# State-matrix powers from size and angle in one pass, parameters loaded ahead of the tokens, a broadcast row loaded behind the weights

## The chip, the cores and the metric

The program runs on one core of a Trainium2 chip. Its engines are PE (TensorE, matrix products; PEld is its weight load), DVE (VectorE), ACT (ScalarE), POOL (GpSimd) and SP (SyncE, which here only issues transfers). Each engine takes its instructions in the order of its own queue, and waits at an instruction until the semaphores it names have come. The metric is device time in microseconds of one execution; lower is better.

## The reference

Two blocks of two layers each run one behind the other on 256 tokens of 1024 channels. The change lies in the first layer, in the mixer with a diagonal state space (S5). What matters of it:

```python
def s5_mixer(u, a_re, a_im, log_dt, b_re, b_im, c_re, c_im, ...):
    dt = jnp.exp(log_dt)[:, None]
    mag = jnp.exp(a_re * dt)
    ab_re = mag * jnp.cos(a_im * dt)
    ab_im = mag * jnp.sin(a_im * dt)
    ...                                   # bb = discretised b, from ab and a
    bu = einsum('blgh,gph->blgp', uf, bb)
    x = associative_scan(x[l] = ab * x[l-1] + bu[l])   # over 256 tokens, complex
    y = einsum('blgp,ghp->blgh', x_re, c_re) - einsum(..., x_im, c_im) + d * uf
    y = gelu(y)
    return y * sigmoid(y @ glu_w + glu_b)

# layer 0
mod = silu(c) @ mod_w[0] + mod_b[0]       # 6 x 1024: shifts, scales, gates
h = rms_norm(x, norm_g[0, 0]) * (1 + sc1) + sh1
proj = h @ ab_w_in                        # 512 columns for S5, 3 x 512 for attention
y = concat([s5_mixer(proj[:, :512]), attention(proj[:, 512:])]) @ ab_w_out
```

There are 32 groups of 64 states (two groups share the 128 partitions, so a state parameter is a tile of 128 x 16), and 16 channels in a group.

## The kernel before

A weight matrix product is computed to nearly fp32: the weight and the operand are split into a rounded part and a remainder (`split`, lines 418 and 419: ACT rounds, DVE subtracts), and PE adds three products, lines 443 to 445. The weights come in loads of 512 KB on SP's queue into a ring of five buffers (`raw`). PE's wide products are what fills most of the time.

The scan is not run token by token. Tokens are taken in blocks of 8. `ssm_params` makes, from the powers 0 to 8 of the state matrix, the matrices that lead from the tokens of a block to its end state (`tt_`, made from `st` by transposes, line 982), from the state before a block to its outputs (`qr`, `qi`), and from a block's tokens to its outputs (`kmat`, by way of a table `ktab` that goes out to memory and back on POOL's queue, lines 1010 and 1014, in eight transfers). `ssm` runs the recursion over the 32 block states in seven steps, on DVE (real part) and POOL (imaginary part), lines 1078 to 1082: three steps inside groups of four blocks, three that double the distance, and one that brings the result to all; they use the powers 8, 16, 24, 32, 64 and 128. Each half of a step waits for the other engine's half of the step before. `ssm_out` multiplies `X`, the states, with `qr` and `qi` (line 1113) and the tokens with `kmat` (line 1110), and brings the outputs back into order (line 1121); gelu and the gated product follow.

The modulation of the first layer is a product of PE with 16 loads of 512 KB (`modulation`, line 543), in two halves of eight; loads go by turns into `raw` and a ring of three, `mraw`. After each half its transposes (line 563) and a reduction (line 570) give shift and scale, `scaled` makes from the tokens the operand (`n`, line 718; its rounded part `hh`, line 722; its remainder `hl`, line 723), and PE multiplies the half of the S5 columns of `ab_w_in` with it. The later parts of the modulations are taken by DVE as sums over rows (`dotted_with`, line 517): a row of weights on each partition times `crow`, which is silu(c) broadcast to all partitions. `row` loads `crow` (512 KB on SP's queue, line 505) and puts silu on it (line 506, ACT, with its table load).

The order on each queue is set by a scheduler that works on the program as it is written, with its own model of times; `issue_after` holds what stands in it behind a named instruction, and SP's order is that of the program in the front. The front writes: the load of the first parameters (`par0`), the tokens (`xT`), the state parameters (`par2`), the identity; squares and sums of the tokens for the norm (lines 705, 710, 638), the rsqrt chain on DVE (lines 646 to 651) and its spread by PE (line 657); then `ssm_params` in pieces between the halves of the modulation.

Of the kernel before, what the change touches and what calls it, by code (L numbers as in the profile page):

```python
# [11 lines left out]
F32 = mybir.dt.float32  # L12
F32R = mybir.dt.float32r
I32 = mybir.dt.int32
AF = mybir.ActivationFunctionType
ALU = mybir.AluOpType
# [3 lines left out]
P = 128  # L20
# [333 lines left out]
class Net:  # L354
# [514 lines left out]
    def ssm_params(self, sp, spt):  # L869

        nc, d, dram = self.nc, self.d, self.dram
        G = 16
        v = nc.vector
        S = [P, G]

        def small(name):
            return spt.tile(S, F32, name=name)
# [4 lines left out]
        lr, li, mag, th = small("s_lr"), small("s_li"), small("s_mag"), small("s_th")  # L882
        v.tensor_tensor(lr, are, dt, op=ALU.mult)
        nc.scalar.activation(mag, lr, AF.Exp)
        v.tensor_tensor(li, aim, dt, op=ALU.mult)
        self.reduce_arg(th, li, S, "s_ra", spt)
        sn, cs, ab = small("s_sn"), small("s_cs"), small("s_ab")
        nc.scalar.activation(sn, th, AF.Sin)
        v.scalar_tensor_tensor(ab, th, -1.0, th, op0=ALU.mult, op1=ALU.max)
        v.tensor_scalar(ab, ab, -1.0, math.pi / 2, op0=ALU.mult, op1=ALU.add)  # L890
        nc.scalar.activation(cs, ab, AF.Sin)

        pr = sp.tile([P, 14, G], F32, name="pr")
        pi = sp.tile([P, 14, G], F32, name="pi")
        v.memset(pr[:, 0, :], 1.0)
        v.memset(pi[:, 0, :], 0.0)
        v.tensor_tensor(pr[:, 1, :], mag, cs, op=ALU.mult)
        v.tensor_tensor(pi[:, 1, :], mag, sn, op=ALU.mult)

        def cmul(o, n, a, b):  # L900

            t1 = self.t([P, 4, G], "s_t1", 1, pool=spt)[:, :n, :]
            br_, bi_ = (q[:, b : b + 1, :].to_broadcast([P, n, G]) for q in (pr, pi))
            ar_, ai_ = pr[:, a : a + n, :], pi[:, a : a + n, :]
            v.tensor_tensor(pr[:, o : o + n, :], ar_, br_, op=ALU.mult)
            v.tensor_tensor(t1, ai_, bi_, op=ALU.mult)
            v.tensor_tensor(pr[:, o : o + n, :], pr[:, o : o + n, :], t1, op=ALU.subtract)
            v.tensor_tensor(pi[:, o : o + n, :], ar_, bi_, op=ALU.mult)
            v.tensor_tensor(t1, ai_, br_, op=ALU.mult)
            v.tensor_tensor(pi[:, o : o + n, :], pi[:, o : o + n, :], t1, op=ALU.add)  # L910

        cmul(2, 1, 1, 1)
        cmul(3, 2, 1, 2)
        cmul(5, 4, 1, 4)
        cmul(9, 1, 8, 8)
        cmul(10, 2, 8, 9)
        cmul(12, 1, 11, 11)
        cmul(13, 1, 12, 12)
# [1048 lines left out]
```

## Time and profile before

| | before |
|---|---|
| time, median of 3 runs | 1439.99 us (1439.74 to 1444.86) |
| the profiled execution | 1446.99 us |
| its span, first to last instruction | 1445.0 us |
| mean granted clock of PE in it | 0.973 of full speed |
| PE busy | 1361.3 us (94%) |
| PEld, DVE, ACT, POOL busy | 1238.6, 1184.4, 837.5, 151.1 us |
| transfers | 311.88 MB, mean 216 GB/s |

All views are of that one execution, times counted from its first instruction. A row in order of time gives start, duration, engine, line, operation, tiles written and read with their shape, how often, and in brackets how long the engine had been idle before and who ended that. A row of the waits names who waited, who was waited for, and the total, the times and the longest in us. The granted clock is a share of full speed.

### The profile page before, as it was taken

How to read it: one execution, taken by the hardware profiler on the slowest of the kernel's cores; microseconds unless marked ns; L12 is line 12 of the kernel's file. 1: busy time of each engine (PE TensorE's matmuls, PEld its weight loads, DVE VectorE, ACT ScalarE, POOL GpSimd, SP SyncE). 2: the span in 40 equal slices, each digit the busy share in tenths (PEclk: the TensorE clock that was granted, in tenths of full speed). 3: DMA queues.
4: the chain of work that ended last, by engine and by line, in shares of the span. 5: the costliest groups of instructions: out<-in, count | busy, mean ns of one | idle time of the engine just before them, and what ended most of it. 6: DMA issues, size and time to landing. Idle time of an engine off the chain costs nothing.

```text
span 1445.0 us, 28181 instructions
## 1 busy us (share of the span) xinstructions
PE 1361.3 (94%) x10702; PEld 1238.6 (86%) x10702; DVE 1184.4 (82%) x2379; ACT 837.5 (58%) x1562; POOL 151.1 (10%) x204
## 2 busy tenths in 40 slices
PE   6988899999998899999989999999999899999997
PEld 3666799999995898999977779999999668999997
DVE  7967888878697697888769867999888978799954
ACT  5533676554474575665457645866556645776642
POOL 1053000101000000001004650000110000000000
PEclk9998999999998999999989999999999899999998
DMA  9567576888757558878635435577795556557660
GB/s 367 205 158 277 202 262 220 277 256 289 245 175 291 177 175 338 277 233 266 213 95 161 137 119 198 155 244 247 264 325 195 170 182 240 176 177 235 193 185 29
DMA packets 91988, 311.88 MB, mean 216 GB/s; under 512 B 10949, under 2 KB 13662, under 8 KB 91726
## 3 DMA queue, kind: packets, MB, share of 16 engines
q1 hardware_dynamic: 72830, 244.67, 50.7%
q0 software_dynamic: 17856, 64.36, 13.9%
q8 instruction: 84, 1.38, 0.4%
q10 hardware_dynamic: 1168, 1.06, 0.3%
q14 instruction: 50, 0.41, 0.1%
HBM read 308.73 MB, written 1.32 MB: 215 GB/s over the span
## 4 chain that ended last, share of the span: by engine, by line
PE 68%; issue 15%; DVE 10%; ACT 3%; DMA 3%; POOL 1%; DVEq 0%; SPq 0%; POOLq 0%; ACTq 0%
PE mm L443 18%; PE mm L445 18%; PE mm L444 18%; DVE lo L419 3%; PE mo L543 2%; ACT hi L418 1%; PE o L1565 1%; PE ax L1665 1%; DVE mraw L517 1%; DMA raw<-ab_in 1%; PE sx L638 1%; PE s L443 1%; PE s L444 1%; POOL mraw L515 1%; PE s L445 1%
## 5 line engine op out<-in xcount | busy, mean ns | idle before, releaser
L418 ACT ACTIVATE hi<-raw 128x1024 fp32r<-128x1024 f32 (+3 forms) x402 | 404.0, 1007 | 371.4 <-PE mm L444 285.4
L419 DVE TENSOR_TENSOR lo<-raw,hi 128x1024 fp32r<-128x1024 f32 (+3 forms) x402 | 464.1, 1161 | 121.3 <-ACT hi L418 119.5
L443 PE MATMUL mm<-hh,hi 128*128 128x256 f32 x1440 | 410.3, 288 | 14.0 <-ACT hi L418 6.4
L445 PE MATMUL mm<-hh,lo 128*128 128x256 f32 x1440 | 407.9, 285 | 5.7 <-DVE lo L419 5.7
L444 PE MATMUL mm<-hl,hi 128*128 128x256 f32 x1440 | 408.3, 285 | 1.6 <-DVE hl L1184 1.0
L443 PEld LDWEIGHTS mm<-hh,hi 128*128 128x128 f32 x1440 | 274.1, 192 | 34.7 <-issue 9.9
L445 PEld LDWEIGHTS mm<-hh,lo 128*128 128x128 f32 x1440 | 275.6, 192 | 8.4 <-DVE lo L419 6.7
L444 PEld LDWEIGHTS mm<-hl,hi 128*128 128x128 f32 x1440 | 275.5, 191 | 7.6 <-issue 3.6
L443 PE MATMUL mm<-ah,hi 128*128 128x256 f32 x704 | 199.1, 283 | 1.8 <-ACT hi L418 1.8
L445 PE MATMUL mm<-ah,lo 128*128 128x256 f32 x704 | 198.0, 282 | 2.2 <-DVE lo L419 2.0
L444 PE MATMUL mm<-al,hi 128*128 128x256 f32 x704 | 197.1, 281 | 0.0
L443 PE MATMUL mm<-zh,hi 128*128 128x258 f32 x608 | 173.7, 289 | 8.1 <-ACT zh L303 4.7
L515 POOL DMA_DIRECT2D mraw<-modt x120 | 64.1, 534 | 1096.1 <-DVE mraw L517 949.1
L445 PE MATMUL mm<-zh,lo 128*128 128x258 f32 x608 | 174.6, 288 | 0.9 <-DVE lo L419 0.7
L444 PE MATMUL mm<-zl,hi 128*128 128x258 f32 x608 | 174.0, 287 | 0.0
L517 DVE SCALAR_TENSOR_TENSOR mraw<-mraw,crow 128x1024 f32<-128x1024 f32 x120 | 145.9, 1226 | 5.7 <-DMA mraw<-modt 5.5
L445 PEld LDWEIGHTS mm<-ah,lo 128*128 128x128 f32 x704 | 132.5, 189 | 3.9 <-DVE lo L419 3.6
L443 PEld LDWEIGHTS mm<-ah,hi 128*128 128x128 f32 x704 | 132.8, 189 | 3.2 <-ACT hi L418 2.0
L444 PEld LDWEIGHTS mm<-al,hi 128*128 128x128 f32 x704 | 132.7, 189 | 1.0 <-issue 1.0
L443 PEld LDWEIGHTS mm<-zh,hi 128*128 128x128 f32 x608 | 117.1, 194 | 9.0 <-ACT zh L303 4.9
L445 PEld LDWEIGHTS mm<-zh,lo 128*128 128x128 f32 x608 | 117.2, 193 | 1.8 <-DVE lo L419 1.7
L444 PEld LDWEIGHTS mm<-zl,hi 128*128 128x128 f32 x608 | 117.9, 194 | 0.2 <-DVE zl L304 0.2
(427 smaller groups left out, 2119.8 us busy)
## 6 DMA issues: line engine op xcount, KB each, us to landing
raw<-up SPq DMA_DIRECT2D x132, 512.0 KB, 4.4
mraw<-modt POOLq DMA_DIRECT2D x120, 512.0 KB, 5.2
raw<-down SPq DMA_DIRECT2D x64, 512.0 KB, 4.4
raw<-mod SPq DMA_DIRECT2D x60, 512.0 KB, 5.2
raw<-gate SPq DMA_DIRECT2D x44, 512.0 KB, 4.7
raw<-down SPq DMA_DIRECT2D x32, 384.0 KB, 3.3
raw<-hy_in SPq DMA_DIRECT2D x24, 512.0 KB, 4.3
raw<-cm_in SPq DMA_DIRECT2D x16, 512.0 KB, 3.6
```

Source lines behind the costliest of these rows:

```text
L418: nc.scalar.activation(hi, src, AF.Copy)
L419: return nc.vector.tensor_tensor(lo, src, hi.bitcast(F32), op=ALU.subtract)
L443: nc.tensor.matmul(out, wh, xh, start=start, stop=False)
L444: nc.tensor.matmul(out, wh, xl, start=False, stop=False)
L445: self.last = nc.tensor.matmul(out, wl, xh, start=False, stop=stop)
L515: nc.gpsimd.dma_start(w, self.d[f"modt{layer}"][u])
L517: nc.vector.scalar_tensor_tensor(w, w, 1.0, row, op0=ALU.mult, op1=ALU.mult, accum_out=out[:, u : u + 1]))
L543: nc.tensor.matmul(acc[g * 32 : g * 32 + 32, :], wt, src, start=(g not in begun), stop=last)
L638: last = self.nc.tensor.matmul(st[:, c0 + t : c0 + t + 1], q[:, t * P : (t + 1) * P], self.ones[:, 0:1], start=(i == 0), stop=(i == len(sq ...
L1565: nc.tensor.matmul(o[i * 64 : i * 64 + 64], vals[:, k, c : c + 64], pt[i][:, k, :], start=(k == 0), stop=(k == 3))
L1665: nc.tensor.matmul(ps, m[:, k, m0 : m0 + P], src[:, k, s], start=(k == 0), stop=(k == 1))
```

## The change

The powers of the state matrix: before, the first power is made of size and angle (`mag`, `th`, 16 columns), and the others of it by complex products (`cmul`, seven calls of six DVE instructions). After, a table of the fourteen exponents is filled on POOL, size and angle of all powers are taken at once (224 columns, in the two buffers that `st1` uses later), and one exp, one reduction of the angle, one sine, one cosine and two products give them all. The state parameters (`par2`) are now loaded ahead of the tokens. `row(0)` stands behind the last modulation load that has been issued, `self.load`, where before it had no such hold.

```diff
--- before.py
+++ after.py
@@ -879,43 +879,31 @@
         are, aim = self.parall("ssm_a_re"), self.parall("ssm_a_im")
         dt = small("s_dt")
         nc.scalar.activation(dt, self.parall("ssm_log_dt"), AF.Exp)
-        lr, li, mag, th = small("s_lr"), small("s_li"), small("s_mag"), small("s_th")
+
+        powers = (0, 1, 2, 3, 4, 5, 6, 7, 8, 16, 24, 32, 64, 128)
+        N = len(powers)
+        kp = spt.tile([P, N], F32, name="s_kp")
+        for i, k in enumerate(powers):
+            nc.gpsimd.memset(kp[:, i : i + 1], float(k))
+        pr = sp.tile([P, N, G], F32, name="pr")
+        pi = sp.tile([P, N, G], F32, name="pi")
+        lr, li = small("s_lr"), small("s_li")
         v.tensor_tensor(lr, are, dt, op=ALU.mult)
-        nc.scalar.activation(mag, lr, AF.Exp)
         v.tensor_tensor(li, aim, dt, op=ALU.mult)
-        self.reduce_arg(th, li, S, "s_ra", spt)
-        sn, cs, ab = small("s_sn"), small("s_cs"), small("s_ab")
+        two = [self.t([P, 4, 8, 16], f"st1{n}", 2, pool=spt).rearrange("p a r h -> p (a r h)") for n in range(2)]
+        mag, th, sn, cs = (t[:, i * N * G : (i + 1) * N * G].rearrange("p (k g) -> p k g", g=G) for t in two for i in range(2))
+        each = lambda q: q[:, None, :].to_broadcast([P, N, G])
+        kb = kp[:, :, None].to_broadcast([P, N, G])
+        v.tensor_tensor(cs, kb, each(li), op=ALU.mult)
+        v.tensor_tensor(mag, kb, each(lr), op=ALU.mult)
+        nc.scalar.activation(mag, mag, AF.Exp)
+        self.reduce_arg(th, cs, [P, N, G], "s_ra", spt)
         nc.scalar.activation(sn, th, AF.Sin)
-        v.scalar_tensor_tensor(ab, th, -1.0, th, op0=ALU.mult, op1=ALU.max)
-        v.tensor_scalar(ab, ab, -1.0, math.pi / 2, op0=ALU.mult, op1=ALU.add)
-        nc.scalar.activation(cs, ab, AF.Sin)
-
-        pr = sp.tile([P, 14, G], F32, name="pr")
-        pi = sp.tile([P, 14, G], F32, name="pi")
-        v.memset(pr[:, 0, :], 1.0)
-        v.memset(pi[:, 0, :], 0.0)
-        v.tensor_tensor(pr[:, 1, :], mag, cs, op=ALU.mult)
-        v.tensor_tensor(pi[:, 1, :], mag, sn, op=ALU.mult)
-
-        def cmul(o, n, a, b):
-
-            t1 = self.t([P, 4, G], "s_t1", 1, pool=spt)[:, :n, :]
-            br_, bi_ = (q[:, b : b + 1, :].to_broadcast([P, n, G]) for q in (pr, pi))
-            ar_, ai_ = pr[:, a : a + n, :], pi[:, a : a + n, :]
-            v.tensor_tensor(pr[:, o : o + n, :], ar_, br_, op=ALU.mult)
-            v.tensor_tensor(t1, ai_, bi_, op=ALU.mult)
-            v.tensor_tensor(pr[:, o : o + n, :], pr[:, o : o + n, :], t1, op=ALU.subtract)
-            v.tensor_tensor(pi[:, o : o + n, :], ar_, bi_, op=ALU.mult)
-            v.tensor_tensor(t1, ai_, br_, op=ALU.mult)
-            v.tensor_tensor(pi[:, o : o + n, :], pi[:, o : o + n, :], t1, op=ALU.add)
-
-        cmul(2, 1, 1, 1)
-        cmul(3, 2, 1, 2)
-        cmul(5, 4, 1, 4)
-        cmul(9, 1, 8, 8)
-        cmul(10, 2, 8, 9)
-        cmul(12, 1, 11, 11)
-        cmul(13, 1, 12, 12)
+        v.scalar_tensor_tensor(th, th, -1.0, th, op0=ALU.mult, op1=ALU.max)
+        v.tensor_scalar(th, th, -1.0, math.pi / 2, op0=ALU.mult, op1=ALU.add)
+        nc.scalar.activation(cs, th, AF.Sin)
+        v.tensor_tensor(pr, mag, cs, op=ALU.mult)
+        v.tensor_tensor(pi, mag, sn, op=ALU.mult)
 
         nr, den, cr, ci, t = small("s_nr"), small("s_den"), small("s_cr"), small("s_ci"), small("s_t")
         v.tensor_scalar(nr, pr[:, 1, :], 1.0, None, op0=ALU.subtract)
@@ -1766,9 +1754,9 @@
         with self.tc.tile_pool(name="sp", bufs=1, reuse_waits="tile") as sp:
             ut = sp.tile([P, 4, T], F32, name="ut")
             with self.tc.tile_pool(name="spt", bufs=1, reuse_waits="tile") as spt, self.banks(mm=4, ax=1, s=1):
-                nc.sync.dma_start(x, d["xT"])
                 self.p2 = spt.tile([P, d["par2"].shape[1]], F32, name="p2")
                 nc.sync.dma_start(self.p2, d["par2"])
+                nc.sync.dma_start(x, d["xT"])
                 nc.sync.dma_start(self.ident, d["k_ident"])
                 sq = []
                 for k in range(DC):
@@ -1812,7 +1800,8 @@
                     for _ in params:
                         pass
             self.later(0, self.modulation(0, range(4, 7), cs, mods[:1]), 1.5)
-            row = self.row(0)
+            with self.tc.issue_after(self.load.ins):
+                row = self.row(0)
             self.pace(1.0)
             self.also(1, 0, 28, 40, row, mods[0])
             self.p1 = per.tile([P, d["par1"].shape[1]], F32, name="p1")
```

The scheduler places the rest anew. ACT, between the two halves of the modulation; `tt_` is the copy of a transposed table, `modsb` that of the modulation, `hh` the rounded operand. Before:

```order
L983 ACTIVATE tt__290<-s 128x8x64
L418 ACTIVATE hi<-raw 128x1024
L560 ACTIVATE modsb<-mo 128x512
L983 ACTIVATE tt__290<-s 128x8x64
L418 ACTIVATE hi<-raw 128x1024
L983 ACTIVATE tt__290<-s 128x8x64 x2
L722 ACTIVATE hh<-n,mod_78 128x256 x3
L418 ACTIVATE hi<-raw 128x1024
L722 ACTIVATE hh<-n,mod_78 128x256
```

After (line numbers are smaller by 12 here):

```order
L971 ACTIVATE tt__253<-s 128x8x64
L560 ACTIVATE modsb<-mo 128x512
L418 ACTIVATE hi<-raw 128x1024
L971 ACTIVATE tt__253<-s 128x8x64
L418 ACTIVATE hi<-raw 128x1024
L971 ACTIVATE tt__253<-s 128x8x64
L506 ACT_TABLE_LOAD
L506 ACTIVATE crow<-crow 128x1024
L971 ACTIVATE tt__253<-s 128x8x64
L722 ACTIVATE hh<-n,mod_78 128x256 x4
```

The row's table load and its silu, which before stand behind the copies of the powers in the front (22 and 23 in ACT's queue), are ahead of the last table copy and the four `hh` of the second half.

POOL, around the eight transfers of `kmat`; `tx` is the recursion's product, 128x128 its first three steps, 128x16x7 the fourth. Before:

```order
L1079 TENSOR_TENSOR tx_956<-X,pi 128x128
L1078 TENSOR_TENSOR tx_956<-X,pr 128x128
L1014 DMA kmat<-kd 16x32x128
L1014 DMA kmat<-kd 16x32x112
L1014 DMA kmat<-kd 16x32x96
L1014 DMA kmat<-kd 16x32x80
L1014 DMA kmat<-kd 16x32x64
L1014 DMA kmat<-kd 16x32x48
L1014 DMA kmat<-kd 16x32x32
L1014 DMA kmat<-kd 16x32x16
L1080 TENSOR_TENSOR tx_956<-tx_956 128x128
L515 DMA mraw<-modt 128x1024 x3
```

After:

```order
L1068 TENSOR_TENSOR tx_919<-tx_919 128x128
L1070 TENSOR_TENSOR X<-X,tx_919 128x16x8
L1067 TENSOR_TENSOR tx_919<-X,pi 128x16x7
L1002 DMA kmat<-kd 16x32x128
L1002 DMA kmat<-kd 16x32x112
L1002 DMA kmat<-kd 16x32x96
L1002 DMA kmat<-kd 16x32x80
L1002 DMA kmat<-kd 16x32x64
L1002 DMA kmat<-kd 16x32x48
L1002 DMA kmat<-kd 16x32x32
L1002 DMA kmat<-kd 16x32x16
L1066 TENSOR_TENSOR tx_919<-X,pr 128x16x7
```

The third step's last two operations (`tx`, then `X`) are ahead of the transfers; before, they stand behind these and three row loads.

PE, in the attention of the first layer, ahead of the state's products; `ssb` and `pt` are softmax tiles, `mm` an accumulator of wide products. Before:

```order
L1219 MATMUL ax<-ident,ssb 128x128 x3
L443 MATMUL mm<-hh,hi 128x256
L444 MATMUL mm<-hl,hi 128x256
L1228 MATMUL o<-pt,vals 64x256
L1228 MATMUL o<-pt,vals 64x128 x2
L443 MATMUL mm<-hh,hi 128x256
L444 MATMUL mm<-hl,hi 128x256
L445 MATMUL mm<-hh,lo 128x256
```

After:

```order
L1207 MATMUL ax<-ident,ssb 128x128 x3
L443 MATMUL mm<-hh,hi 128x256
L444 MATMUL mm<-hl,hi 128x256
L1216 MATMUL o<-pt,vals 64x256
L1101 MATMUL sx<-qr,X 32x128 x4
L1101 MATMUL sx<-qi,X 32x128 x4
L1098 MATMUL sx<-kmat,u_623 32x128 x4
L1101 MATMUL sx<-qr,X 32x128 x4
L1101 MATMUL sx<-qi,X 32x128 x4
L1098 MATMUL sx<-kmat,u_623 32x128 x4
```

Before, 34 wide products lie between and the first product with `X` is row 447; after, it is row 414, and these wide products follow it.

## Rows read from the trace of the kernel before

**Rows 1.** Busy us (instructions) of PE, PEld, DVE, ACT, POOL, then PEclk, DMA, GB/s

```profile
100.00:200.00 100.00, 85.94 (x760) 71.37 (x753) 75.83 (x170) 51.87 (x113) 20.06 (x31) 0.91 0.76 257
200.00:300.00 100.00, 98.69 (x827) 98.28 (x827) 90.26 (x158) 66.44 (x119) 6.33 (x12) 1.00 0.74 240
```

**Rows 2.** In order of time, DVE: start, us, line, operation, tiles, idle before

```profile
9.75 0.43 DVE L710 TENSOR_TENSOR n<-n 128x256 f32<-128x256 f32 x1
...
13.39 0.17 DVE L905 TENSOR_TENSOR pr<-pr 128x16 f32<-128x16 f32 x1
...
19.34 0.15 DVE L651 SCALAR_TENSOR_TENSOR ny<-nu,ny 128x2 f32<-128x2 f32 x1
...
25.28 0.19 DVE L570 TENSOR_REDUCE mod<-ax 128x8 f32<-128x32 f32 x1
25.39 0.17 DVE L910 TENSOR_TENSOR pi<-pi,s_t 128x16 f32<-128x16 f32 x1
...
26.92 1.66 DVE L718 SCALAR_TENSOR_TENSOR n<-x,a,sx 128x256 f32<-128x256 f32 x4
```

**Rows 3.** In order of time, PE, the front

```profile
22.25 0.66 PE L982 MATMUL s<-ident,st 128*128 128x128 f32 x4 [0.99 <-DVE st L965]
22.84 1.05 PE L543 MATMUL mo<-raw,cs 128*32 128x512 f32 x4
...
30.16 0.38 PE L444 MATMUL mm<-hl,hi 128*128 128x256 f32 x1 [0.45 <-DVE hl L723]
```

**Rows 4.** In order of time, ACT, the front

```profile
6.26 1.03 ACT L705 ACTIVATE n<-x 128x256 f32<-128x256 f32 x3 [2.39 <-DMA x<-xT]
...
19.14 1.28 ACT L506 ACT_TABLE_LOAD   x1
20.44 1.06 ACT L506 ACTIVATE crow<-crow 128x1024 f32<-128x1024 f32 x1
...
43.30 1.30 ACT L722 ACTIVATE hh<-n,mod 128x256 fp32r<-128x256 f32 x3
```

**Rows 5.** In order of time, SP's queue, the front

```profile
10.97 0.35 SPq L505 DMA_DIRECT2D crow<-c_rows  x1
12.33 0.33 SPq L553 DMA_DIRECT2D mraw<-mod  x1
```

**Rows 6.** The chain that ended last: start, us, what, around 100 us

```profile
92.79 12.60 DMA raw<-ab_in
```

**Rows 7.** In order of time, POOL, the recursion's third and fourth step

```profile
104.70 0.63 POOL L1082 TENSOR_TENSOR X<-X,tx 128x128 f32<-128x128 f32 x1
...
106.78 1.42 POOL L1082 TENSOR_TENSOR X<-X,tx 128x112 f32<-128x112 f32 x1
```

**Rows 8.** In order of time, DVE, the recursion's last step

```profile
121.65 1.72 DVE L1078 TENSOR_TENSOR tx<-X,pr 128x336 f32<-128x336 f32 x1
...
127.37 0.49 DVE L1082 TENSOR_TENSOR X<-X,tx 128x336 f32<-128x336 f32 x1
```

**Rows 9.** In order of time, PE, ahead of the state's products and these

```profile
120.45 0.86 PE L1228 MATMUL o<-pt,vals 128*64 128x256 f32 x6 [0.41 <-ACT pt L1221]
...
131.19 0.42 PE L1113 MATMUL sx<-qr,X 64*32 64x128 f32 x8
```

**Rows 10.** Who waited for whom, PE, 100 to 160: us, times, longest

```profile
PE mm L443 <- ACT hi L418: 4.2, 1, 4.2
PE mm L445 <- DVE lo L419: 2.7, 1, 2.7
PE ax L1219 <- ACT pt L1221: 1.9, 1, 1.9
PE ax L1219 <- DVE ssb L1216: 1.8, 2, 0.9
PE o L1228 <- ACT pt L1221: 1.3, 3, 0.6
PE sx L1121 <- ACT y L1122: 0.5, 1, 0.5
```


## The prediction

> **What bounds the kernel now.** I read first the busy time by stretch, then each engine in order of time over the first 160 us, then who PE waited for there. From 200 us on PE is the bound: 98.69 us busy of 100 between 200 and 300, at granted clock 1.00 [rows 1]. An edit that neither lengthens nor shortens PE's work can win nothing there; it can only hand that part over earlier or later. Between 100 and 200 us PE is busy 85.94 of 100 and the clock is 0.91 [rows 1]. So the change has to be judged in its first 160 us, by what PE waits for.
>
> In the front PE waits for products of DVE: the transposes of the first state table stand ahead of the last modulation product in PE's queue, and wait 0.99 us for DVE [rows 3]. That product, at 22.84, closes the first modulation; its reduction comes at 25.28, the scaled tokens at 26.92, and the first wide product with both halves at 30.16 [rows 2, 3]. The rsqrt chain that needs the tokens ends at 19.34 [rows 2], seven microseconds before anything asks for it, so it isn't what ends last.
>
> **The powers.** Removed are seven complex products of six instructions, 42 on DVE, from 13.39 (the first) to 25.39 (the last) [rows 2], spread between other work, 0.17 us of record each at 16 columns. Added are twelve instructions of 224 elements in place of thirteen of 16: two scalings by the table of exponents, six for the reduction of the angle, two for the cosine's argument and two products. The nearest row is one of 256 elements, 0.43 us [rows 2]; twelve of these are 5.2 us as an upper bound, and 2.0 us, twelve times the 0.17 of a 16 wide one [rows 2], the lower one. I take the upper, since 224 is close to 256. Most of these run while ACT and DVE wait for the tokens, because the parameters now come first. On ACT one table load less stands in the front. The fourteen small fills on POOL run before the parameters can land, on an engine that has nothing else to do there: cost nothing, and a few tenths if it had.
>
> **Parameters ahead of the tokens.** The parameters are 540 KB. Two loads of 512 KB are 1.36 us apart in the queue when it runs full [rows 5], so the tokens come about 1.4 us later: squares from 7.7 instead of 6.26 [rows 4]. The squares must also pass the load for the sine and the waits on the reduced angle between them, by the new order, so I have the sums finished at 15.6. After these the rsqrt chain stands in one piece on DVE, without the powers between its steps: eleven dependent steps at 0.2 us end at 18.9, against 19.34 [rows 2]. Nothing is won or lost there. What is won lies behind it: no powers are left between the table's products, so these end at about 22.6, the reduction of the modulation comes at 23.8 (25.28 before) and the wide products start at 28.15 (30.16 before) [rows 2, 3]: **minus 2.0 us**, and minus 0.5 if the sums are 1.5 later than I have them.
>
> **The row for sums.** Its transfer left its place ahead of two modulation loads, which land up to 1.36 us earlier [rows 5]; the last product of the first modulation was not waiting for them but for DVE, so this alone is worth nothing. Its table load and activation leave a hole on ACT at 19.14 and 20.44, 1.28 and 1.06 us [rows 4], and now stand ahead of the last table copy and the four roundings of the second half (the order on ACT, above). Those roundings began at 43.30 [rows 4]. With the first half 2.0 earlier and 2.34 us in front of them they begin at 43.30 - 2.0 + 2.34 = 43.6: the front as a whole gives **plus 0.35 us**. The ends are minus 2.0 (ACT would have idled there anyway) and plus 2.3 (the first half gains nothing). Queued behind the row on ACT are that table copy, the roundings and the next weight split; PE waits for the roundings, DVE for their remainders.
>
> The ACT rows show the load for 1.28 us and the activation starting 0.02 us after its end [rows 4]. The Trainium skill (ScalarE: Activation LUTs, section What ACT_TABLE_LOAD costs) counts a drain of 1380 ns beside the 1283 ns of the load; these rows show none behind the load. By the page the roundings would begin at 45.0 and the sum would be 1.4 us longer; I go by the rows.
>
> **Order behind the front.** Three places moved with it. On POOL the last addition of the recursion's third step ran at 104.70, behind the eight matrix transfers, and the fourth step's at 106.78 [rows 7]. In the new order the third stands ahead of the transfers, so one step less is left behind them: 2.1 us. On DVE the last addition of the recursion stood behind two weight splits, an attention remainder and score work: from 121.65 to 127.37 [rows 8], of which only the first 1.72 us is the recursion's. It is now ahead of them: 4.0 us. Together the state is complete at 127.37 + 0.49 - 4.0 - 2.1 = 121.8. On PE the products that read it ran at 131.19 and now stand directly behind the row of 120.45 that ends at 121.3 [rows 9]: a wait of 0.5 us. The 34 wide products that stood between come after. The gain is in what follows. PE waited 1.9, 1.8, 1.3 and 0.5 us for softmax and output transposes between 100 and 160 us [rows 10], where it had run out of wide products. With those products still in hand and the output chain started some nine microseconds earlier, I take 4.0 of these 5.5 us back, less the 0.5 spent: **minus 3.5 us**. Bounds: minus 5.5, and plus 3.9 if the state is no earlier (below). The waits of 4.2 and 2.7 us for weights [rows 10] I leave as they are. Later stages are also reordered in places, with equal instructions; with PE at 98.69 of 100 I put 0, within 1.5 either way: 1.3 us of that stretch is all that PE could win.
>
> Sum: 0.35 - 3.5 = -3.15 us. Against the profiled execution, 1446.99 us with a span of 1445.0, that is 1443.8; that execution lies 7 us above the median of the runs shown, 1439.99, so on the median the forecast is **1436.8 us**, no difference beyond 0.5% (7.2 us), which is about what a measurement of this kernel can tell from none.
>
> **Rivals.** *The state is no earlier.* PE meets its products at 121.3 [rows 9] and the state is complete at 127.86 [rows 8]: 6.6 us of idling, of which the 2.7 us wait for weights [rows 10] is saved since these land meanwhile. That is +3.9 with the fillers not taken back, and the clock, 0.91 already [rows 1], may fall further after it: about 1444.5, at most 1449. It decides from the point where the state comes after 125.3, when the wait eats the 4.0 I took back. For it: DVE is the engine with work queued in that stretch, and a step on POOL still waits for the transfers. Against: both orders moved the recursion forward.
>
> *The hole at 102 closes.* PE's longest wait, 4.2 us, ends with a weight load that took 12.60 us [rows 6, 10] while the matrix transfers ran. These now stand three POOL operations later; if the weight load goes ahead of them, the 4.2 us go too: 1436.8 - 4.2 = 1432.6, and down to 1429 with the clock of that stretch restored. Against: both share the same transfer engines whichever comes first, and the state's products then wait longer.
>
> *It does not do what it says.* The front's transfers run back to back, loads are gated by buffers that PE frees, and the row costs on ACT what the powers gave: the front is where it was, and the later order changes nothing on balance: 1440.3.
>
> **How the numbers follow.** Forecast 0.45 (1433 to 1440; 0.04 of it below 1432.8), no earlier state 0.17 (1442 to 1449; 0.07 above 1447.2), the hole closes 0.18 (1428 to 1433; 0.15 below 1432.8), nothing 0.20 (1438 to 1443). Faster 0.04 + 0.15 = 0.19; slower 0.07; within 0.5% 0.74. The range 1430 to 1444 leaves out about 0.1 on either side.
>
> **What would show it.** Right: wide products starting near 28 us; the row's activation on ACT near 42 with the roundings just behind; the state's last addition on DVE near 122 and PE's products on it at once; fewer than 3 us of PE waits for softmax and output between 100 and 160. Wrong: the sums on PE ending after 17; the state after 125; a changed wait for weights at 102; or a difference that arises after 200 us.

## The result, and the profile after

| | before | after |
|---|---|---|
| time, median of 5 runs each, same chip | 1440.98 us (1439.74 to 1445.86) | 1455.85 us (1453.33 to 1461.56) |
| the profiled execution | 1446.99 us | 1461.56 us |
| its span | 1445.0 us | 1459.6 us |
| sums of the second norm on PE, line 638 | 189.71 us | 201.84 us |

The changed kernel takes 1.0087 times as long (95 % interval 1.0061 to 1.0113; the two medians by themselves differ by 1.0 %): slower by 0.9 %, where 1436.8 us and no difference were forecast. The profiled executions are 14.6 us apart, as the medians are (14.9), and each lies about 6 us above its median, so the two traces can be compared as they stand. Of these 14.6 us, 12.1 have arisen by the sums of the second norm, the first work that needs all of the first mixer.

First the whole stretch up to these sums, before and then after (columns as in [rows 1]):

```profile
0.00:189.71 189.71, 158.20 (x1380) 118.37 (x1380) 151.00 (x364) 93.19 (x190) 40.40 (x64) 0.95 0.73 244
```

```profile
0.00:201.84 201.84, 166.95 (x1382) 124.33 (x1382) 148.05 (x322) 91.66 (x189) 39.44 (x78) 0.89 0.69 227
```

PE runs the same number of products. It is busy 8.75 us longer with them, and idle 3.38 us longer (201.84 - 166.95 = 34.89 against 31.51). The mean granted clock is 0.89 instead of 0.95. So under a third of the loss is waiting, and the rest is the same work on a slower clock. DVE is the engine that the powers relieve: it runs 42 instructions fewer and is busy 3 us less, and nothing is won by that.

Then PE in order of time, at the places where the two traces part, first before and then after:

```profile
43.85 0.73 PE L443 MATMUL mm<-hh,hi 128*128 128x256 f32 x4 [1.08 <-ACT hh L722]
...
106.53 0.58 PE L443 MATMUL mm<-hh,hi 128*128 128x256 f32 x1 [4.18 <-ACT hi L418]
...
124.56 0.58 PE L445 MATMUL mm<-hh,lo 128*128 128x256 f32 x1 [2.66 <-DVE lo L419]
```

```profile
28.55 0.39 PE L444 MATMUL mm<-hl,hi 128*128 128x256 f32 x1
...
44.32 1.23 PE L443 MATMUL mm<-hh,hi 128*128 128x256 f32 x4 [2.59 <-ACT hh L722]
...
93.12 0.51 PE L443 MATMUL mm<-hh,hi 128*128 128x256 f32 x1 [2.11 <-DVE qk L419]
...
114.46 0.58 PE L443 MATMUL mm<-hh,hi 128*128 128x256 f32 x1 [4.78 <-ACT hi L418]
...
128.54 0.65 PE L1101 MATMUL sx<-qr,X 64*32 64x128 f32 x8
...
158.09 0.88 PE L1207 MATMUL ax<-ident,ssb 128*128 128x128 f32 x3 [3.32 <-DVE ssb L1204]
...
201.84 0.95 PE L638 MATMUL sx<-ones,n 128*128 128x1 f32 x8
```

The wide products start 1.6 us earlier than in [rows 3]. Then the lead turns. The modulation product ahead of the first scores starts at 89.94, before at 87.31 (+2.6). The first scores are at 101.68 against 95.74 (+5.9). The wait for weights ends at 114.46 against 106.53 (+7.9), and the sums come at +12.1. So four stretches cost 2.6, 3.3, 2.0 and 4.2 us. In the last of them, from the wait for weights to the sums, PE waits less than before, not more (before, then after):

```profile
106.53:189.71 83.18, 73.33 (x651) 59.98 (x651) 66.08 (x142) 43.12 (x92) 16.65 (x25) 0.90 0.71 246
```

```profile
114.46:201.84 87.38, 78.60 (x653) 63.19 (x653) 63.04 (x138) 43.38 (x93) 12.36 (x18) 0.83 0.66 227
```

PE is idle 8.78 us there against 9.85, and busy 5.27 us longer, at a clock of 0.83 against 0.90.

From 200 us on PE is bound as in [rows 1] (busy 98.69 us between 200 and 300 again). Behind 900 us comes a wait that the trace of before lacks; the same product of before, then of after, and the 40 us around it in after:

```profile
886.59 0.28 PE L443 MATMUL mm<-zh,hi 128*128 128x258 f32 x1
```

```profile
903.62 0.36 PE L443 MATMUL mm<-zh,hi 128*128 128x258 f32 x1 [2.88 <-DVE x L754]
```

```profile
880.00:920.00 40.00, 34.77 (x276) 32.82 (x277) 29.29 (x59) 21.89 (x40) 0.58 (x1) 1.00 0.58 182
```

These 2.9 us are of the size of the rest (14.6 - 12.1 = 2.5), though the two traces don't add up so neatly: after is 14.2 us late just ahead of this wait, 17.0 behind it, and 14.6 at the end, so some 2 us came and went in other places. No fall of the clock follows this wait: it is 1.00 from 880 to 920.

### The profile page after: what moved, and what is told of

Read it like the earlier page. It is cut to its first block, busy times and chain, and to the rows that moved or that the text cites. A ratio compares the mean times of both kernels' runs of the same rounds, so it can differ in the third digit from the quotient of the medians.

```text
span 1459.6 us, 28149 instructions
## 1 busy us (share of the span) xinstructions
PE 1364.6 (93%) x10702; PEld 1243.2 (85%) x10702; DVE 1180.2 (81%) x2337; ACT 838.3 (57%) x1561; POOL 149.1 (10%) x218
## 4 chain that ended last, share of the span: by engine, by line
PE 71%; issue 13%; DVE 8%; DMA 4%; ACT 3%; POOL 1%; SPq 0%; DVEq 0%; POOLq 0%; ACTq 0%
PE mm L443 19%; PE mm L444 19%; PE mm L445 19%; DVE lo L419 2%; PE mo L543 2%; DMA raw<-ab_in 2%; PE o L1553 1%; DVE mraw L517 1%; PE ax L1653 1%; ACT hi L418 1%; PE s L443 1%; PE sx L638 1%; PE s L444 1%; PE s L445 1%; DMA raw<-mod 1%
```

## Experiments

Each run was timed beside the kernel before on its own chip (medians 1443.66, 1442.23, 1442.78 and 1442.45 us for e1 to e4, e5 to e8, e9 to e12 and e13 to e16). "Sums" is the start of the second norm's sums in the run's profile, 189.71 before. One execution says this to within about 4 us only: e10 and e13 run the same instructions up to there and have 190.01 and 194.19, after and e14 201.84 and 198.83. Of the 4.2 us between e10 and e13, 2.4 are PE busy longer, at a mean granted clock of 0.91 instead of 0.93. So the ratios decide, and the sums say where.

### Which part costs the time

The theory: the row's activation between the halves of the modulation, and the order behind it. The rival: the powers, or parameters that delay the tokens. e1 is before with the powers alone, so after with two pieces undone:

```diff
+                nc.sync.dma_start(x, d["xT"])
                 self.p2 = spt.tile([P, d["par2"].shape[1]], F32, name="p2")
                 nc.sync.dma_start(self.p2, d["par2"])
-                nc.sync.dma_start(x, d["xT"])
...
-            with self.tc.issue_after(self.load.ins):
-                row = self.row(0)
+            row = self.row(0)
```

> The kernel before with the powers alone made in one pass; tokens and row as before. In this program the row's activation stands on ACT in the idle time of the front again, and on DVE a product of the fifth step of the recursion, which reads what POOL adds in the fourth, stands ahead of the remainder of the first scores. Theory 'the order behind the front': the edit itself is worth nothing within 1 us up to the second half of the first wide products (first of them at 43.9 plus or minus 1, half of the clock gone by 49), but PE then waits for that remainder as in the changed kernel (2.11 us there) or up to 2 us longer, the granted clock falls behind the wait, and the program ends at 1444 to 1456. Rival 'the powers cost': the wide operations and their table of exponents delay the front, so that the wide products start after 31 us, and the end is late by about what the front is late. Rival 'the row alone': without the row's move there is no loss, 1438 to 1443.

e2 is before with the exchange of the two loads alone, e3 before with the row's hold alone:

```diff
-                nc.sync.dma_start(x, d["xT"])
                 self.p2 = spt.tile([P, d["par2"].shape[1]], F32, name="p2")
                 nc.sync.dma_start(self.p2, d["par2"])
+                nc.sync.dma_start(x, d["xT"])
```

> The kernel before with the parameters loaded ahead of the tokens, nothing else. The tokens come some 1.4 us later, which no step that ends last asks for: the first wide product at 30.2 plus or minus 1 and the second half as before. The row stays early. Behind the front the order on DVE and POOL has the fifth step's product ahead of the first scores' remainder, as with the powers alone. Theory 'the order behind the front': 1444 to 1456, about what the powers alone give, though the edits have nothing in common but the order. Rival 'the loads cost': only this kernel and those that share the edit are late, from the first sums on. Rival 'the row alone': 1438 to 1443.

```diff
-            row = self.row(0)
+            with self.tc.issue_after(self.load.ins):
+                row = self.row(0)
```

> The kernel before with the row alone moved behind the modulation loads. The row's table load and activation (1.28 and 1.06 us) stand on ACT just ahead of the roundings of the second half; without the 1.5 us that the changed kernel had won by then I expect the roundings at 45 and the second half's products some 1.5 us later than in the changed kernel, with the same fall of the clock behind. Behind the front the DVE order is nearly that of the changed kernel (fourth step's product ahead of the first scores' remainder). Theory 'the order behind the front', and 'the row alone' too: 1452 to 1460. A rival by which powers or parameters make the loss has this one at 1438 to 1446.

e4 is after with the powers made as before (the first piece of the diff undone):

```diff
-        powers = (0, 1, 2, 3, 4, 5, 6, 7, 8, 16, 24, 32, 64, 128)
...
+        cmul(2, 1, 1, 1)
...
+        cmul(13, 1, 12, 12)
```

> The changed kernel with the powers made by complex products as before. From the front on, PE's order is that of the changed kernel, row by row. Theory 'the order behind the front': as slow as the changed kernel, 1452 to 1460, with PE's wait for the first scores' remainder at 2 us and the hole before the next weights of 4 to 5. Rival 'the powers cost': 1440 to 1446.

| run | median us | ratio (95 %) | sums |
|---|---|---|---|
| e1 powers alone | 1445.95 | 1.0018 (1.0000 to 1.0036) | 185.44 |
| e2 parameters first alone | 1448.78 | 1.0032 (1.0009 to 1.0055) | 191.58 |
| e3 row alone | 1455.61 | 1.0092 (1.0068 to 1.0116) | 199.76 |
| e4 both loads moved, old powers | 1455.66 | 1.0080 (1.0052 to 1.0108) | 200.32 |

The row's move alone is enough for the whole loss, and with the old powers it is the same. e1 and e2 came out in the range that the order behind the front was to give, but not by its wait: in neither does PE wait for the first scores' remainder. What they have in common with after is the wait behind 900 us (the last group below). ACT of e3, the first rounding:

```profile
47.15 0.50 ACT L722 ACTIVATE hh<-n,mod 128x256 fp32r<-128x256 f32 x1
```

Without the lead of the powers the roundings come 3.85 us behind [rows 4].

### Which places of the new order cost it

e5 holds the row's silu behind the four roundings `hh`. e6 holds the recursion's doubling steps, line 1067, behind the remainder of the first scores' operand. e7 is both.

```diff
-        self.nc.scalar.activation(c, c, AF.Silu)
+        with self.tc.issue_after(self.held.ins):
+            self.nc.scalar.activation(c, c, AF.Silu)
...
-                nc.scalar.activation(hi[:, k, :], t, AF.Identity, bias=sh[:, k : k + 1])
+                self.held = nc.scalar.activation(hi[:, k, :], t, AF.Identity, bias=sh[:, k : k + 1])
```

> The changed kernel with one move: the row's table load and activation (1.28 and 1.06 us on ACT) stand behind the four roundings of the second half instead of ahead of them; every other instruction of every engine is where it was. Theory 'the row's place on ACT' (it is this delay that starts the loss: the wait of 2.59 us for the roundings and the half clock from 42 to 52 behind it): roundings at 41.4 instead of 43.8, PE's wait for them under 1 us, the half clock of the second half down from 10.2 us to at most 4, PE 2.5 to 4 us ahead of the changed kernel at 80, and the end 2.5 to 8 us earlier, 1448 to 1453. Rival 'the order behind the front': the lead is eaten by the waits behind (first scores' remainder, weights at 110, score rows at 125 and 158), and the end is within 1.5 us of the changed kernel's, 1454 to 1457. Rival 'the whole loss': 1440 to 1444.

```diff
-            step(X4[:, :, :, s:, 3:4], X4[:, :, :, : 8 - s, 3:4], 11 + k, 1)
+            with self.tc.issue_after(self.scored.ins):
+                step(X4[:, :, :, s:, 3:4], X4[:, :, :, : 8 - s, 3:4], 11 + k, 1)
...
-                    else:
+                    elif c:
                         self.split(*o[1], acc)
+                    else:
+                        self.scored = self.split(*o[1], acc)
```

> The changed kernel with one move on DVE: the fourth step of the recursion (its products, the first of which waits 2.68 us for POOL) stands behind the two remainders of the first scores instead of ahead of them; everything else is where it was. Theory 'the order behind the front': PE's wait of 2.11 us for the remainder shrinks to 0.3, the half clock behind it (93 to 97) goes, and PE is 3.3 us ahead of the changed kernel at 95; at the end 2 to 4 us are left, 1451 to 1453.5. Rival 'the row's place on ACT': the waits of the transfers behind absorb it, end within 1.5 us of the changed kernel.

> Both moves, otherwise the changed kernel. If the two causes are independent the gains add: by the two theories together 6 to 11 us earlier than the changed kernel, 1444 to 1450. If PE's later waits set the end, no better than the better of the two. What stays above 1443 then belongs to the order of score and state work from 110 to 165 us, which neither move touches.

e8 leaves before as it is, the row's transfer too, and holds only its silu back, behind the fourth weight rounding:

```diff
+        self.rounded.append(rounded)
...
-        self.nc.scalar.activation(c, c, AF.Silu)
+        with self.tc.issue_after(self.rounded[3].ins):
+            self.nc.scalar.activation(c, c, AF.Silu)
```

> The kernel before with the row's transfer where it was, on SP's queue as before, and its table load and activation alone held behind the last weight rounding of the front, ahead of the roundings of the second half. Theory 'the row's place on ACT': PE waits 2 to 3 us more ahead of the second half, the clock is half for 7 to 10 us there, and the end is 4 to 12 us late, 1447 to 1456 (the order behind the front becomes much like that of the changed kernel). Rival 'the row's transfer' (what costs is the place of its 512 KB among the modulation loads): as before, 1441 to 1446.

| run | median us | ratio (95 %) | sums |
|---|---|---|---|
| e5 row behind the roundings | 1451.48 | 1.0053 (1.0033 to 1.0073) | 195.21 |
| e6 step behind the scores | 1451.73 | 1.0057 (1.0038 to 1.0075) | 197.13 |
| e7 both | 1449.03 | 1.0044 (1.0024 to 1.0063) | 196.87 |
| e8 silu alone late | 1450.94 | 1.0056 (1.0037 to 1.0074) | 193.30 |

By the ratios e5 takes 0.0034 and e6 0.0030 off after's 1.0087, 4 to 5 us each, which is at the edge of what the intervals can tell apart from nothing; e7 takes off 0.0043, less than the sum of the two, though the intervals don't rule out that they add up. The stretch behind PE's first wait, of before, after and e5:

```profile
42.00:53.00 11.00, 9.81 (x58) 8.15 (x59) 11.00 (x20) 6.29 (x13) 0.00 (x0) 0.84 0.69 261
```

```profile
42.00:53.00 11.00, 8.68 (x37) 7.18 (x38) 10.06 (x19) 5.54 (x11) 0.00 (x0) 0.54 0.43 171
```

```profile
42.00:53.00 11.00, 10.23 (x53) 8.43 (x53) 11.00 (x21) 7.96 (x14) 0.00 (x0) 0.69 0.42 167
```

PE waits 2.59 us in after, and the clock that it is then granted is 0.54, mostly the 1.2 GHz level: 37 products where before has 58. In e5 it waits 1.08 us (at 42.77), is granted 0.69 and does 53. Before waits the same 1.08 us (at 43.85) and is granted 0.84, so the length of this one wait doesn't settle the clock behind it.

In e8 the transfer stands where it stood, and most of the loss is there (1.0056, against 1.0092 for e3): so much comes with the activation's place on ACT, without the transfer's. What the rest belongs to isn't shown. PE waits there for a table copy behind the silu:

```profile
44.66 1.12 PE L986 MATMUL s<-ident,st 128*128 128x128 f32 x4 [3.15 <-ACT tt__290 L987]
```

DVE of after at the second place, then of e6:

```profile
90.81 0.51 DVE L1067 TENSOR_TENSOR tx<-X,pi 128x112 f32<-128x112 f32 x1 [2.68 <-POOL X L1070]
91.21 1.21 DVE L419 TENSOR_TENSOR lo<-raw,hi 128x1024 fp32r<-128x1024 f32 x1
...
92.56 0.41 DVE L419 TENSOR_TENSOR qk<-mm,qk 128x256 fp32r<-128x256 f32 x1
```

```profile
88.57 0.42 DVE L419 TENSOR_TENSOR qk<-mm,qk 128x256 fp32r<-128x256 f32 x1
...
92.36 0.34 DVE L1067 TENSOR_TENSOR tx<-X,pi 128x112 f32<-128x112 f32 x1
```

In after the product of the fourth step waits 2.68 us for POOL, with a weight remainder and the scores' remainder `qk` queued behind it. PE has nothing else and waits 2.11 us for `qk` (before 0.33), then runs its products at 0.41 us instead of 0.28 until 96.4. With the step held behind `qk`, 0.3 us of that wait are left.

### The end of the attention, and the order without the row's move

What stays of e7 lies behind 106 us, and there the state's products now run: its wait for weights ends at 105.67, before's at 106.53. e9 writes them one pair of heads later, behind all but four of the wide products; e10 has the edits of e5, e6 and e9.

```diff
+        self.wides.append(self.last)
...
-                if c == 1:
-                    with self.tc.issue_after(self.last.ins):
+                if c == 2:
+                    with self.tc.issue_after(self.wides[-5].ins):
                         yc, yh, yl = self.ssm_out(sp, ap, u2)
```

> The changed kernel with the state's output products (with the matrices, and with the states) written behind the wide products of the last scores: on PE they follow 46 of these, where the kernel before had them behind 35, and the changed kernel ahead of all but 2. Theory 'the state's products too early' (what I forecast as the gain is a loss: small products run while the granted clock is half, from 127 to 141, and the gelu of their result shares DVE with the softmax of the last scores, for which PE then waits 3.32 us with no wide product left): half clock between 110 and 180 us down from 31 us to under 18, the wait for the last softmax under 2 us, PE 3 to 5 us ahead of the changed kernel at 200, end 1450 to 1453.5. Rival 'waits only move': the score chain ends when it did, PE within 1.5 us of the changed kernel at 200, end 1454 to 1457.

> The changed kernel with all three moves: the row's activation behind the roundings, the recursion's fourth step behind the first scores' remainders, the state's output products behind the wide products. If these three are what made the changed kernel slow, the rest of the change is worth nothing and the end is that of the kernel before within 3 us, 1440 to 1445.5. If what is left in the kernel with two moves (1449.0 against 1442.2) sits elsewhere, 1447 to 1451.

e11 is after without the row's move, e12 this with the edits of e6 and e9:

```diff
-            with self.tc.issue_after(self.load.ins):
-                row = self.row(0)
+            row = self.row(0)
```

> The changed kernel with the row loaded where it was: powers in one pass and parameters first alone. Theory 'the row's place' (its move is the change's loss): 1441 to 1449, as powers alone and parameters alone gave 1446 and 1449; the wide products start 1 to 2 us earlier and the second half keeps that lead. Rival 'each edit costs a little' (plus 2.3 and plus 5.1 against the kernel before add up): 1449 to 1452.

> Powers in one pass and parameters first, the row where it was, and the two moves behind the front (fourth step behind the first scores' remainders, state's output products behind the wide products). With the front's lead of 1 to 2 us kept and the order behind it as in the kernel before, the theory gives 1437 to 1442, at or a little ahead of the kernel before; a rival by which the lead is swallowed by the transfers before 110 us gives 1442 to 1446.

| run | median us | ratio (95 %) | sums |
|---|---|---|---|
| e9 state's products later | 1449.55 | 1.0039 (1.0012 to 1.0065) | 194.31 |
| e10 all three | 1446.67 | 1.0020 (1.0000 to 1.0039) | 190.01 |
| e11 after without the row's move | 1446.92 | 1.0032 (1.0011 to 1.0054) | 190.31 |
| e12 e11 with two of the edits | 1453.38 | 1.0079 (1.0051 to 1.0108) | 196.88 |

The state's products in before, in after and in e9:

```profile
131.00:141.00 10.00, 10.00 (x207) 5.95 (x207) 3.80 (x7) 1.99 (x4) 1.10 (x2) 1.00 0.60 191
```

```profile
126.00:142.00 16.00, 15.35 (x136) 9.45 (x140) 8.65 (x25) 5.95 (x18) 0.77 (x2) 0.57 0.64 215
142.00:152.00 10.00, 10.00 (x147) 7.34 (x148) 4.23 (x9) 4.44 (x9) 0.53 (x1) 1.00 0.26 72
```

```profile
126.00:142.00 16.00, 15.96 (x175) 11.25 (x173) 10.44 (x27) 6.53 (x19) 1.20 (x3) 0.89 0.84 286
```

In before they follow wide products at the clock's upper level (0.42 us for eight, [rows 9]). In after they follow two waits, of 1.64 and 0.40 us, and take 0.65 us for eight, with PE busy 15.35 of 16 us at a mean clock of 0.57. The wide products from 136 to 140 us are in this stretch too, at 0.41 us each; from 141.9 the state's products take 0.42 us for eight again, and the clock is 1.00. In e9 the same wait of 1.64 us, and one of 0.21, have wide products behind them; these run at 0.41 us up to 129.3, and the clock of the stretch is 0.89. e9 trades this for a wait of 4.6 us for the gelu's result, so it isn't free. PE of e9, in order of time, then that wait:

```profile
124.06 0.88 PE L1209 MATMUL ax<-ident,ssb 128*128 128x128 f32 x3 [1.64 <-DVE ssb L1206]
...
129.33 0.37 PE L445 MATMUL mm<-hl,hi 128*128 128x256 f32 x1
```

```profile
PE mm L444 <- ACT yhl L419: 4.6, 1, 4.6
```

e12 is the miss of this group. The two edits that help the order of after hurt the one without the row's move; PE waits 6.06 us at 111.27 for a softmax tile:

```profile
111.27 1.10 PE L1212 MATMUL ax<-ident,ssb 128*128 128x128 f32 x3 [6.06 <-DVE ssb L1209]
```

What makes DVE so late there was not followed up. e10 lies between its two forecasts (1440 to 1445.5 if the three places are all, 1447 to 1451 if something else is left).

### What is left: the wait behind 900 us

The three edits bring e10 back to 1.0020, and e1 has its sums 4 us earlier than before while its median gains nothing. Both have a wait that before lacks; e10's:

```profile
890.06 0.55 PE L444 MATMUL mm<-zh,hi 128*128 128x258 f32 x1 [2.86 <-DVE x L757]
```

It is there in after and in e1 to e12, 2.2 to 2.9 us each. A new ring of accumulators is opened in that stage. The theory is that in before its first product writes another bank than the one that DVE still reads (line 754 of after), and in the others the same one; the traces name no banks. One filled column takes a bank of the ring and so turns this round: e13 is e10 with it, e14 after, e15 e11, e16 e1.

```diff
         e.enter_context(self.banks(mm=4, ax=2))
+        v.memset(self.mm()[:, :1], 0.0)
         self.dump("x4", x)
```

> The kernel with all three moves, and one small fill on DVE more, which only makes the products at the head of the fourth stage's first feed-forward take another accumulator bank; every other instruction stands where it was. In the kernel before these products start without a wait (their bank was read long before); in each of the thirteen changed kernels profiled they wait 2.2 to 2.9 us near 890 us for DVE to read the product just ended, since the two banks of the stage ahead come out swapped. Theory 'the bank': that wait goes, with the half clock behind it, 2.5 to 4.5 us, so 1442 to 1444.5, equal to the kernel before within 2 us. Rival 'the wait moves on': 1445 to 1448, as without the fill.

> The changed kernel with the fill alone. Theory 'the bank': 2 to 4.5 us earlier than the changed kernel, 1451 to 1454, the wait near 903 gone. Rival 'the wait moves on': within 1 us of the changed kernel, 1455 to 1457.

> Powers in one pass and parameters first, the row where it was, with the fill. Without the fill 1446.9. Theory 'the bank': 1442 to 1444.5. Rival: 1446 to 1448.

> The powers alone with the fill. Without it 1446.0, with 2.2 us of wait at that place. Theory 'the bank': 1441 to 1444, at or ahead of the kernel before, since PE met the sums of the next norm 4.3 us earlier there in the one execution profiled. Rival: 1445 to 1447.

| run | median us | ratio (95 %) | sums |
|---|---|---|---|
| e13 three edits and the fill | 1442.79 | 0.9995 (0.9975 to 1.0016) | 194.19 |
| e14 after and the fill | 1449.54 | 1.0051 (1.0029 to 1.0072) | 198.83 |
| e15 without the row's move, and the fill | 1443.79 | 1.0009 (0.9993 to 1.0024) | 187.67 |
| e16 powers alone, and the fill | 1446.14 | 1.0018 (0.9997 to 1.0039) | 185.09 |

In none of the four is more than 0.2 us of the wait left; in e14:

```profile
PE mm L443 <- DVE x L754: 0.2, 1, 0.2
```

The median of e14 is 6.3 us below after's, more than the 2.7 us that the wait lost and more than was forecast; the two intervals overlap, so the rest is not read as an effect. With the four places undone e13 stands where before stands. Taken singly they give 4.4, 4.1, 6.3 and 6.3 us on the medians, 21 in all where 13.1 were lost: they don't add up, and how much each weighs alone isn't settled. No version beat before: e15, the powers and the parameters first without the row's move, is level with it.

e16 is a miss: its wait of 2.2 us is gone, and its ratio is the 1.0018 of e1, where 1441 to 1444 us were forecast. The powers alone have their sums over 4 us earlier in both profiled executions (185.44 and 185.09), but these are not typical ones. That of e16 took 1435.30 us, the shortest of its twelve and 10.8 below its median, and its lead grew to 11.6 us at the end; that of before lies about 6 us above its median. So whether the powers alone give a lead at all isn't shown, and why e16 gains nothing on e1 stays open.

## Why the prediction was wrong

**Powers and parameters: right, one step by luck.** Squares were forecast from 7.7 and begin at 7.74, sums ended by 15.6 and end at 15.4, the rsqrt chain ends at 19.3 (18.9), the reduction comes at 24.20 (23.8), the wide products at 28.55 (28.15). DVE of after:

```profile
12.80 0.39 DVE L905 TENSOR_TENSOR pr<-st,st 128x224 f32<-128x224 f32 x1
...
24.20 0.18 DVE L570 TENSOR_REDUCE mod<-ax 128x8 f32<-128x32 f32 x1
```

The 224 wide product took 0.39 us, and the twelve together 4.2, nearer to the upper bound of 5.2 than to 2.0. The end of the rsqrt chain fits by luck: eleven steps of 0.2 us behind 15.6 end at 17.8, not at 18.9. The steps did take 0.2 us, but the chain began only at 17.16, behind other work on DVE. Nothing hung on it. The wide products came 1.6 us earlier instead of 2.0.

**The row on ACT: the size was right, what PE does behind it was left out.** ACT of after:

```profile
41.04 1.28 ACT L506 ACT_TABLE_LOAD   x1
42.33 1.06 ACT L506 ACTIVATE crow<-crow 128x1024 f32<-128x1024 f32 x1
43.30 0.58 ACT L971 ACTIVATE tt__253<-s 128x512 f32<-128x512 f32 x1
43.77 1.70 ACT L722 ACTIVATE hh<-n,mod 128x256 fp32r<-128x256 f32 x4
```

The roundings begin at 43.77 (forecast 43.6; by the same sum with the 1.6 us that came, 44.0), and again no row shows a drain: the silu starts 0.01 us behind the load and the next copy as soon as the silu ends. What the Trainium skill counts beyond the load (ScalarE: Activation LUTs, section What ACT_TABLE_LOAD costs) isn't seen at this place either. But the step "the front as a whole gives plus 0.35 us" took the start of the second half for its end. The lead of the first half does not pay for the 2.34 us: PE reaches the wait earlier, stands 2.59 us, and is then granted 0.54 of its clock. By the modulation product ahead of the first scores it is 2.6 us later than before.

**The recursion moved forward: the queues behind its waits were left out.** The forecast counted what stood ahead of the recursion in the new order, not what the recursion was put ahead of. On DVE its fourth step waits for POOL with the first scores' remainder behind it (above, 3.3 us with the clock). On POOL the third step did come 14.6 us earlier, at 90.14. The fourth did not:

```profile
90.14 0.63 POOL L1070 TENSOR_TENSOR X<-X,tx 128x128 f32<-128x128 f32 x1
92.82 4.99 POOL L1002 DMA_DIRECT2D kmat<-kd  x8 [1.66 <-DMA kd<-ktab]
97.82 1.22 POOL L1066 TENSOR_TENSOR tx<-X,pr 128x112 f32<-128x112 f32 x1
102.78 0.61 POOL L515 DMA_DIRECT2D mraw<-modt  x1 [3.74 <-DVE at L419]
107.04 0.55 POOL L515 DMA_DIRECT2D mraw<-modt  x1 [3.65 <-DVE ssb L1204]
108.86 0.53 POOL L515 DMA_DIRECT2D mraw<-modt  x1 [1.28 <-DMA kmat<-kd]
...
110.01 0.56 POOL L1070 TENSOR_TENSOR X<-X,tx 128x112 f32<-128x112 f32 x1
```

Between the fourth step's two products stand the eight transfers, and between its second product (97.82) and its addition (110.01) three row loads, which wait 3.74, 3.65 and 1.28 us for other things. The step ends at 110.57, where before it ended at 108.20 [rows 7]. The term "one step less is left behind the transfers: 2.1 us" failed here, and with it the 121.8:

```profile
127.42 0.51 DVE L1070 TENSOR_TENSOR X<-X,tx 128x336 f32<-128x336 f32 x1
```

The state is complete at 127.93, before at 127.86 [rows 8].

**The fillers: the sign was wrong.** PE does not stand before the state's products, because it comes there late: the row ahead of them runs at 127.50, not 120.45 [rows 9]. Up to 136 us they run at the lower clock level, and the wide products that they were put ahead of don't fill the softmax waits. PE's waits of after between 100 and 165:

```profile
PE ax L1207 <- DVE ssb L1204: 5.0, 2, 3.3
PE mm L443 <- ACT hi L418: 4.8, 1, 4.8
PE o L1216 <- ACT pt L1209: 1.4, 2, 1.0
PE mo L543 <- DMA raw<-mod: 0.6, 1, 0.6
PE ax L1207 <- ACT pt L1209: 0.2, 1, 0.2
```

For softmax and output PE waits 6.6 us, not under 3 and not the 5.5 of [rows 10]. The output chain that started earlier comes in the way on DVE: its gelu stands between the parts of the last softmax, whose reduction is at 155.48 and whose result for PE at 157.68.

```profile
155.48 0.42 DVE L1199 TENSOR_REDUCE smax<-ssb 128x1 f32<-128x256 f32 x1
...
156.99 0.69 DVE L1122 SCALAR_TENSOR_TENSOR yc<-yc,y 128x512 f32<-128x512 f32 x1
157.68 0.53 DVE L1204 TENSOR_SCALAR ssb<-ssb,sinv 128x128 f32<-128x128 f32 x2
```

Instead of minus 3.5 us, the stretch from the first scores to the sums gave plus 6.2 (12.1 - 5.9). Almost none of that is waiting: up to the end of the wait for weights PE idles 1.2 us more than before, and behind it 1.1 us less, where the 2.7 us wait for a weight remainder is gone (below). What grew is the time of the same products, on the slower clock.

**The waits for weights** were both left as they are. The longer one nearly is: 4.78 against 4.2 us [rows 10], moved along with PE; the rival that it closes fell. The shorter one, 2.7 us in before, isn't among the waits of after: the state's products now run ahead of the product that waited there, as the rival "the state is no earlier" had it.

**Later stages: mis-sized.** The 0 within 1.5 us became 2.5. It left out a wait of 2.9 us where a new ring of accumulators begins; the fill that takes it away (e13 to e16) speaks for two neighbouring products on the same accumulator.

**The rivals.** "The state is no earlier" had the right mechanism on POOL and DVE, at plus 3.9 and at most 1449; but PE did not idle for the state, and the clock counted there for a few us only. The clock was the larger part: 8.75 of 12.1 us, with 5.27 of them between the wait for weights and the sums. The sum of the forecast had no term for it.

## What to carry to other kernels

When a new order puts a step ahead, look at what now stands behind that step's waits on each queue it passes; a recursion that goes to and fro between two engines gains only what the slower of both queues lets through. A wait on a bound PE can cost more than its length when the products behind it run at a lower granted clock (0.54 behind the 2.59 us at 44 us, but 1.00 behind the 2.88 us at 903 us): take the price from a stretch of the trace behind such a wait. And when an operation moves from a place where its engine idles to one where PE waits for that engine, the place can weigh more than its 2.3 us (8.7 us between the medians in e8), for the whole order behind it changes too.

## What had not been expected of the hardware

Between 126 and 142 us PE was busy 15.35 of 16 us and yet granted 0.57 of its clock: first with the state's products of 64 rows and 32 columns, then with wide ones. The same state's products had 1.00 in before, behind wide products that had run since 124.56 without a wait. In after the lower level lasts from 127.5 to 141 us; in e9, with wide products behind the same wait of 1.64 us, it is over at 129.3, some 5 us after that wait. So it lasted longer where the small products stood behind that wait; this is one execution each, and the second wait differs (0.40 and 0.21 us). A wait of 2.88 us was followed by no fall of the clock, and one of 1.08 us by 0.84 in before and 0.69 in e5. A wait that a single fill of one column removes cost 2.2 to 2.9 us in a stage 700 us behind the change. And the first 200 us of two executions of one order can end 3 to 4 us apart, with different granted clocks, which is as much as most of the single effects here.
